# Spreading 1/sum of the softmax with a float32r one-hot product in two parts instead of a float32 one

## The chip, the cores and the metric

The kernel runs on one core of one Trainium2 chip, as one program launch. The metric is the device time of that launch in microseconds (us), and a profile is one further execution of the same program.

## The reference, cut to what matters

A hybrid encoder of two layers over 512 tokens of width 1024, then a final RMSNorm. In each layer one input projection feeds a bidirectional SSD (Mamba-2) group and a grouped-query attention group (8 query heads, 2 key/value heads, 64 wide); their outputs are concatenated, go through one output projection and are added to the residual, and a SwiGLU feed-forward follows. What the change touches is the division in the softmax:

```
s = jnp.einsum("bqgrd,bkgd->bgrqk", qi, k)
p = jax.nn.softmax(s, axis=-1)
out = jnp.einsum("bgrqk,bkgd->bqgrd", p, v)
```

The kernel keeps exp(s - max) without the division, multiplies it by v, and divides the 512 x 512 attention output by the row sums at the end.

## The kernel before, in words

Weights and activations are split in a high and a low float32r tile (`whi`, `wlo`, `xh`, `xl`), and a product is three float32r matmuls: high by high (L410), high by low (L411), low by high (L412), 512 columns each. `Stream.split` makes the two weight tiles from each fetched chunk: a cast on ScalarE (L191) and a subtraction on VectorE (L192).

In `mixer` three generators are interleaved: `att` (attention), `fill` (the projections, and `out_half(1)`, the half of the output projection that uses the SSD group's rows) and `ssd`. Attention leaves unnormalized outputs in `qr` and the row sums in `sums` (128 tokens x 4 chunks x 8 heads). When the projections are done, `att` calls `normalize` at high priority:

- `sel`, 8 x 512, has a 1 where column / 64 equals the row, made by GpSimd with a memset (L676) and a select (L678) in a slot of the ring `p_ring`.
- `rec` = 1/sums on VectorE (L681), four transposes on TensorE into a bank `ps_t` (L684), a ScalarE copy to `rows`, 8 x 512 (L686), another slot of `p_ring`.
- For each j of 4, a float32 matmul of a 128-column piece of `sel` by `rows` (L689) spreads 1/sum over 128 partitions into one of two banks `ps_s`. VectorE multiplies `qr` by it (L691), ScalarE casts the product to `xh` (L693), and VectorE subtracts for `xl` (L694, a call of the helper `tt`, so that its records stand under L94).

Then `out_half(0)` multiplies these four row blocks: each output block m takes three matmuls for each of k = 0 to 3, and block k needs the `xh` and `xl` that pass j = k made. Sums leave the two banks `ps_a` by a VectorE addition (L820). The last matmuls of `out_half(1)` and the first of `out_half(0)` stand beside the four passes of `normalize`.

The order in which each engine gets its instructions isn't written by hand: the program is traced with a planner (`schedule_with_timeline_sim=True` at the end of the file) that simulates each engine with its own costs and picks the next instruction by priority and readiness. Each engine then runs its list in order.

Of the kernel before, what the change touches and what calls it, by code (L numbers as in the profile page):

```python
# [15 lines left out]
F32 = mybir.dt.float32  # L16
F32R = mybir.dt.float32r
I32 = mybir.dt.int32
AF = mybir.ActivationFunctionType
ALU = mybir.AluOpType  # L20
# [3 lines left out]
P = 128  # L24
# [3 lines left out]
S = 512  # L28
NC = S // P
# [17 lines left out]
B1, B2, B3, BR = 2, 2, 3, 2  # L47
# [22 lines left out]
def merge(a, b, c):  # L70
    return a.rearrange("p (b c) -> p b c", b=b, c=c)


def bc(ap, shape, axis):
    return ap.unsqueeze(axis).broadcast_to(shape)
# [3 lines left out]
def tile_hybrid_encoder(ctx, tc, xt_d, par_d, rope_d, snw_d, w_kvdt, w_xbc, w_q, w_z, w_out, w_gate, w_up, w_down, out_d):  # L79
    nc = tc.nc  # L80
    V, A, G, T = nc.vector, nc.scalar, nc.gpsimd, nc.tensor
# [11 lines left out]
    def tt(e, *args):  # L93
        (G if e == "G" else V).tensor_tensor(*args)  # L94

    def bank(tag):


        return psum.tile([P, S], F32, name=f"ps_{tag}", tag=tag)
# [151 lines left out]
    ident = const.tile([P, P], F32, name="ident")  # L251
# [184 lines left out]
    def mixer(l, norm, mx):  # L436
# [26 lines left out]
        for c in range(NC):  # L463
            out = A.activation(kvd[:, c], pk[c][:, :KVDT], AF.Copy, scale=rt[:, c:c + 1])  # L464
# [6 lines left out]
        base = mx.tile([P, 2, NC, 64], F32, name="base", tag="t2", bufs=B2)  # L471
# [29 lines left out]
        if l == 0:  # L501
            for t, rows, v in ((segr, (0, 32), 1.0), (segl, (64, 72), -1.0)):
                hot = mx.tile([P, 8], F32, name="hot", tag="qm", bufs=2)
                G.memset(hot, 0.0)
                for r in rows:
                    G.affine_select(out=hot, in_=hot, pattern=[[-1, 8]], compare_op=ALU.not_equal, fill=v,
                                    base=-r, channel_multiplier=1)
# [144 lines left out]
        def ring(which):  # L652
            turn[which] += 1
            return rings[which][:, turn[which] % 4]
# [15 lines left out]
        sums = mx.tile([P, NC, 8], F32, name="sums")  # L670

        def normalize():


            sel = ring("p")[:8]
            G.memset(sel, 0.0)  # L676
            pick = merge(sel, 8, 64)
            G.affine_select(out=pick, in_=pick, pattern=[[-1, 8], [0, 64]], compare_op=ALU.not_equal, fill=1.0,  # L678
                            base=0, channel_multiplier=1)
            rec = mx.tile([P, NC, 8], F32, name="rec")  # L680
            V.reciprocal(rec, sums)  # L681
            tp = bank("t")
            for c in range(NC):
                T.transpose(tp[:8, c * P:(c + 1) * P], rec[:, c], ident)  # L684
            rows = ring("p")[:8]
            A.copy(rows, tp[:8])  # L686
            for j in range(4):
                b = bank("s")
                T.matmul(b, lhsT=sel[:, j * P:(j + 1) * P], rhs=rows, start=True, stop=True)  # L689
                o = qr.rearrange("p c (j a) d -> p j c (a d)", a=2)[:, j]  # L690
                V.tensor_tensor(o, o, merge(b, NC, P), ALU.mult)  # L691
                h = merge(mixed.h[j], NC, P)
                A.copy(h, o)  # L693
                tt(MLE, merge(mixed.l[j], NC, P), o, h.bitcast(F32), ALU.subtract)  # L694
# [191 lines left out]
        def att():  # L886
            todo = [(c, g) for g in range(2) for c in range(NC)]
            ready = None
            for i, (c, g) in enumerate(todo):
                while g not in qri:  # L890
                    yield
                now = ready or queries(c, g)
                ready = None
                if i + 1 < len(todo) and todo[i + 1][1] in qri:
                    ready = queries(*todo[i + 1])
                yield from attention(c, g, *now)
            while "z" not in done:
                yield
            with tc.high_priority():
                normalize()  # L900
            done.append("att")
# [290 lines left out]
```

## Time and profile before

| | us |
|---|---|
| median of 3 runs shown | 1235.92 |
| the three runs | 1235.92, 1230.69, 2627.81 |
| the profiled execution's own time | 1231.69 |
| its span, first to last instruction | 1230.0 |
| TensorE busy | 1198.6 (97%) |
| VectorE busy | 902.4 (73%) |
| ScalarE busy | 630.5 (51%) |
| GpSimd busy | 157.8 (13%) |
| mean granted TensorE clock | 0.990 of full speed |

PE is TensorE's matmuls, PEld its weight loads, DVE VectorE, ACT ScalarE, POOL GpSimd. Matmuls are pipelined, so the duration of one record is longer than the distance from its start to that of the next; the chain of waits counts the distance. A float32 matmul leaves two records, a float32r one a single record. Times in the traces count from the span's start. `normalize` runs once in each layer, near 209 to 244 us and 808 to 843 us.

### The profile page before, as it was taken

How to read it: one execution, taken by the hardware profiler on the slowest of the kernel's cores; microseconds unless marked ns; L12 is line 12 of the kernel's file. 1: busy time of each engine (PE TensorE's matmuls, PEld its weight loads, DVE VectorE, ACT ScalarE, POOL GpSimd, SP SyncE). 2: the span in 40 equal slices, each digit the busy share in tenths (PEclk: the TensorE clock that was granted, in tenths of full speed). 3: DMA queues.
4: the chain of work that ended last, by engine and by line, in shares of the span. 5: the costliest groups of instructions: out<-in, count | busy, mean ns of one | idle time of the engine just before them, and what ended most of it. 6: DMA issues, size and time to landing. Idle time of an engine off the chain costs nothing.

```text
span 1230.0 us, 19740 instructions
## 1 busy us (share of the span) xinstructions
PE 1198.6 (97%) x7718; PEld 1059.6 (86%) x7718; DVE 902.4 (73%) x1475; ACT 630.5 (51%) x1203; POOL 157.8 (13%) x144
## 2 busy tenths in 40 slices
PE   6999999999999999999999999999999999999996
PEld 6788886687899899899898898777879989989985
DVE  6898976457887677677679977856698847847843
ACT  5678675244354254254465776744444623623544
POOL 0203433011100000000202144401020000000002
PEclk9999999999999999999999999999999999999998
DMA  6221212224243234231442111212243333333121
GB/s 224 73 73 48 66 37 68 69 69 142 89 126 120 65 120 126 64 104 39 126 147 91 69 35 61 87 35 69 77 146 112 105 110 95 102 114 95 35 72 75
DMA packets 47534, 110.04 MB, mean 89 GB/s; under 512 B 5425, under 2 KB 5937, under 8 KB 47441
## 3 DMA queue, kind: packets, MB, share of 16 engines
q1 hardware_dynamic: 46720, 107.68, 27.7%
q8 instruction: 60, 0.98, 0.3%
q10 hardware_dynamic: 720, 1.11, 0.3%
q14 instruction: 34, 0.27, 0.1%
HBM read 104.44 MB, written 4.33 MB: 88 GB/s over the span
## 4 chain that ended last, share of the span: by engine, by line
PE 86%; DVE 9%; ACT 2%; issue 1%; DMA 1%; POOL 0%; ACTq 0%; DVEq 0%; POOLq 0%
PE ps_a L1054 6%; PE ps_a L1053 6%; PE ps_a L1052 6%; PE ps_a L410 5%; PE ps_a L411 5%; PE ps_a L412 5%; PE ps_a L1099 3%; PE ps_a L1098 3%; PE ps_a L1100 3%; PE ps_s L1098 3%; PE ps_s L1099 3%; PE ps_s L1100 3%; PE ps_s L1054 3%; PE ps_s L1053 3%; PE ps_s L1052 3%; PE ps_t L717 3%
## 5 line engine op out<-in xcount | busy, mean ns | idle before, releaser
L191 ACT CAST whi<-wraw 128x512 fp32r<-128x512 f32 (+4 forms) x183 | 125.5, 714 | 217.7 <-PE ps_a L411 57.6
L191 ACT CAST whi<-sraw 128x1024 fp32r<-128x1024 f32 x126 | 131.6, 1050 | 141.2 <-DVE sraw L166 40.7
L192 DVE TENSOR_TENSOR wlo<-wraw,whi 128x512 fp32r<-128x512 f32 (+4 forms) x183 | 152.5, 845 | 59.5 <-ACT whi L191 58.4
L192 DVE TENSOR_TENSOR wlo<-sraw,whi 128x1024 fp32r<-128x1024 f32 x126 | 153.5, 1223 | 46.5 <-ACT whi L191 46.3
L410 PE MATMUL ps_a<-xh,whi 128*128 128x512 f32 x320 | 128.3, 405 | 5.5 <-ACT kvd L464 1.7
L411 PE MATMUL ps_a<-xl,whi 128*128 128x512 f32 x320 | 128.2, 402 | 0.0
L412 PE MATMUL ps_a<-xh,wlo 128*128 128x512 f32 x320 | 127.8, 399 | 0.0
L322 POOL TENSOR_TENSOR ssq<-ssq,sqt 128x512 f32<-128x512 f32 x17 | 25.2, 1481 | 671.1 <-ACT sqt L319 670.8
L166 DVE TENSOR_TENSOR sraw<-sraw 128x1024 f32<-128x1024 f32 x72 | 88.0, 1222 | 1.0
L418 PE MATMUL ps_a<-whi,xh 128*128 128x256 f32 (+1 forms) x256 | 74.6, 292 | 9.4 <-ACT xh L306 9.4
L1054 PE MATMUL ps_a<-ss,wlo 128*128 128x256 f32 x288 | 81.7, 284 | 0.0
L1052 PE MATMUL ps_a<-ss,whi 128*128 128x256 f32 x288 | 81.5, 283 | 0.0
L1053 PE MATMUL ps_a<-ss,whi 128*128 128x256 f32 x288 | 81.5, 283 | 0.0
L1054 PE MATMUL ps_a<-s,wlo 128*128 128x256 f32 x288 | 81.1, 283 | 0.0
L1053 PE MATMUL ps_a<-s,whi 128*128 128x256 f32 x288 | 81.1, 283 | 0.0
L410 PEld LDWEIGHTS ps_a<-xh,whi 128*128 128x128 f32 x320 | 61.6, 193 | 22.1 <-ACT s L1013 4.0
L1052 PE MATMUL ps_a<-s,whi 128*128 128x256 f32 x288 | 79.8, 283 | 0.0
L411 PEld LDWEIGHTS ps_a<-xl,whi 128*128 128x128 f32 x320 | 61.4, 192 | 15.5 <-DVE xl L94 1.5
L419 PE MATMUL ps_a<-wlo,xh 128*128 128x256 f32 (+1 forms) x256 | 74.2, 291 | 0.0
L412 PEld LDWEIGHTS ps_a<-xh,wlo 128*128 128x128 f32 x320 | 61.4, 192 | 14.7 <-issue 2.0
L420 PE MATMUL ps_a<-whi,xl 128*128 128x256 f32 (+1 forms) x256 | 72.5, 287 | 0.0
L1098 PE MATMUL ps_s<-hid,whi 128*128 128x512 f32 (+1 forms) x182 | 69.9, 384 | 0.0
(399 smaller groups left out, 3420.4 us busy)
## 6 DMA issues: line engine op xcount, KB each, us to landing
sraw<-in_w_gate SPq DMA_DIRECT2D x72, 256.0 KB, 5.6
sraw<-in_w_up SPq DMA_DIRECT2D x72, 256.0 KB, 4.2
wraw<-in_w_down SPq DMA_DIRECT2D x48, 384.0 KB, 3.5
wraw<-in_w_xbc SPq DMA_DIRECT2D x16, 512.0 KB, 3.3
wraw<-in_w_out SPq DMA_DIRECT2D x16, 512.0 KB, 4.2
wraw<-in_w_q SPq DMA_DIRECT2D x8, 512.0 KB, 3.3
wraw<-in_w_z SPq DMA_DIRECT2D x8, 512.0 KB, 3.4
wraw<-in_w_gate SPq DMA_DIRECT2D x8, 512.0 KB
```

Of the source, the lines that this page charges most:

```text
L166: V.tensor_tensor(q[to], q[to], q[by], ALU.add)
L191: A.copy(hi[:, u], raw[:, u])
L192: (G if lo_pool else V).tensor_tensor(lo[:, u], raw[:, u], hi[:, u].bitcast(F32), ALU.subtract)
L410: T.matmul(ps, lhsT=wh, rhs=op.h[k], start=first, stop=False)
L411: T.matmul(ps, lhsT=wh, rhs=op.l[k], start=False, stop=False)
L412: T.matmul(ps, lhsT=wl, rhs=op.h[k], start=False, stop=last)
L418: T.matmul(ps, lhsT=xh, rhs=wh, start=first, stop=False)
L419: T.matmul(ps, lhsT=xh, rhs=wl, start=False, stop=False)
L1052: T.matmul(out, lhsT=wh[:, o:o + P], rhs=x_[:, 0, i], start=first and i + j == 0, stop=False, skip_group_check=True)
L1053: T.matmul(out, lhsT=wh[:, o:o + P], rhs=x_[:, 1, i], start=False, stop=False, skip_group_check=True)
L1054: T.matmul(out, lhsT=wl[:, o:o + P], rhs=x_[:, 0, i], start=False, stop=i == 3, skip_group_check=True)
L1098: T.matmul(ps[:, cols], lhsT=w1[:, o:o + P], rhs=h, start=f == a, stop=False)
```

## The change

`sel` is built on VectorE as a sum of two broadcast pieces of the identity: rows 0 to 7 and rows 8 to 15 each hold the one-hot pattern, 16 x 512, in float32r, in a buffer of the tag `raw`, which the convolution and the query projection use earlier. 1/sum is split in a float32r part and the rest (`rec` is 128 x 4 x 16): the reciprocal is taken in place, a VectorE copy rounds it, a VectorE subtraction gives the rest. The four transposes give 16 rows instead of 8, the ScalarE copy writes 16 x 512 in float32r into the other `raw` buffer, and the four matmuls at L689 contract 16 rows in float32r. The two GpSimd instructions are gone. Nothing else is edited.

```diff
         def normalize():
-            sel = ring("p")[:8]
-            G.memset(sel, 0.0)
-            pick = merge(sel, 8, 64)
-            G.affine_select(out=pick, in_=pick, pattern=[[-1, 8], [0, 64]], compare_op=ALU.not_equal, fill=1.0,
-                            base=0, channel_multiplier=1)
-            rec = mx.tile([P, NC, 8], F32, name="rec")
-            V.reciprocal(rec, sums)
+            sel = mx.tile([P, S + 4], F32R, name="one", tag="raw", bufs=BR)[:16, :S]
+            V.tensor_tensor(merge(sel, 8, 64), bc(ident[:16, :8], [16, 8, 64], 2), bc(ident[:16, 8:16], [16, 8, 64], 2), ALU.add)
+            rec = mx.tile([P, NC, 16], F32R, name="rec")
+            V.reciprocal(sums, sums)
+            V.tensor_copy(rec[:, :, :8], sums)
+            V.tensor_tensor(rec[:, :, 8:], sums, rec[:, :, :8].bitcast(F32), ALU.subtract)
             tp = bank("t")
             for c in range(NC):
-                T.transpose(tp[:8, c * P:(c + 1) * P], rec[:, c], ident)
-            rows = ring("p")[:8]
-            A.copy(rows, tp[:8])
+                T.transpose(tp[:16, c * P:(c + 1) * P], rec[:, c].bitcast(F32), ident)
+            rows = mx.tile([P, S + 4], F32R, name="rows", tag="raw", bufs=BR)[:16, :S]
+            A.copy(rows, tp[:16])
             for j in range(4):
                 b = bank("s")
                 T.matmul(b, lhsT=sel[:, j * P:(j + 1) * P], rhs=rows, start=True, stop=True)
```

## Rows read from the trace of the kernel before

**Rows 1.** The page, part 1: busy time, share of the span, instructions.
```profile
PE 1198.6 (97%) x7718; PEld 1059.6 (86%) x7718; DVE 902.4 (73%) x1475; ACT 630.5 (51%) x1203; POOL 157.8 (13%) x144
```

**Rows 2.** Windows of both layers: us, busy (count) PE PEld DVE ACT POOL, PEclk, DMA, GB/s.
```profile
235.30:250.30 15.00, 14.67 (x39) 8.22 (x37) 7.79 (x13) 4.11 (x7) 0.00 (x0) 0.77 0.11 36
834.50:847.90 13.40, 13.07 (x39) 7.60 (x37) 7.72 (x13) 4.14 (x7) 0.00 (x0) 0.87 0.12 39
```

**Rows 3.** The chain of waits: start us, us on the chain, what.
```profile
235.67 1.91 PE ps_s L689 x4
...
238.01 0.23 PE ps_a L410
...
238.71 1.05 PE ps_s L689 x2
...
240.19 1.81 PE ps_s L689 x2
...
243.16 0.43 PE ps_a L410
...
834.86 1.91 PE ps_s L689 x4
...
839.38 1.05 PE ps_s L689 x2
```

**Rows 4.** Timeline, TensorE: start us, us, engine, line, operation, out<-in, shapes, count.
```profile
235.60 1.98 PE L689 MATMUL ps_s<-p_ring 8*128 8x512 f32 x4
...
238.31 0.40 PE L412 MATMUL ps_a<-xh,wlo 128*128 128x512 f32 x1
...
243.38 0.63 PE L411 MATMUL ps_a<-xl,whi 128*128 128x512 f32 x1
...
249.50 0.39 PE L412 MATMUL ps_a<-xh,wlo 128*128 128x512 f32 x1
...
834.79 1.98 PE L689 MATMUL ps_s<-p_ring 8*128 8x512 f32 x4
...
841.22 0.63 PE L411 MATMUL ps_a<-xl,whi 128*128 128x512 f32 x1
...
847.08 0.39 PE L412 MATMUL ps_a<-xh,wlo 128*128 128x512 f32 x1
```

**Rows 5.** Timeline, VectorE, same columns; [idle before <-what ended it].
```profile
236.76 0.69 DVE L691 TENSOR_TENSOR qr<-qr,ps_s 128x512 f32<-128x512 f32 x1 [2.17 <-PE ps_s L689]
...
238.83 0.68 DVE L820 TENSOR_TENSOR part<-part,ps_a 128x512 f32<-128x512 f32 x1
...
241.23 0.68 DVE L94 TENSOR_TENSOR xl<-qr,xh 128x512 fp32r<-128x512 f32 x1
...
242.65 1.51 DVE L94 TENSOR_TENSOR xl<-qr,xh 128x512 fp32r<-128x512 f32 x2
...
835.95 0.69 DVE L691 TENSOR_TENSOR qr<-qr,ps_s 128x512 f32<-128x512 f32 x1 [2.18 <-PE ps_s L689]
...
840.42 0.69 DVE L94 TENSOR_TENSOR xl<-qr,xh 128x512 fp32r<-128x512 f32 x1
```

**Rows 6.** Windows in which TensorE's clock was low; columns as in rows 2.
```profile
242.00:246.80 4.80, 4.80 (x13) 3.75 (x12) 1.98 (x3) 0.62 (x1) 0.00 (x0) 0.50 0.33 109
841.20:844.20 3.00, 3.00 (x8) 2.32 (x7) 1.80 (x3) 0.62 (x1) 0.00 (x0) 0.50 0.53 175
```

**Rows 7.** Timeline, TensorE, early in layer 0: the first matmul after a stall.
```profile
32.59 0.80 PE L410 MATMUL ps_a<-xh,whi 128*128 128x512 f32 x1 [1.66 <-ACT kvd L464]
```

**Rows 8.** VectorE, by line and tile (ns min/median/max, first and last start), then one timeline row.
```profile
L681 DVE RECIPROCAL rec<-sums x2: 353/353/353, 210.9 to 808.7; 128x32 f32<-128x32 f32 x2
...
L94 DVE TENSOR_TENSOR H<-H,EX x8: 681/1054/1342, 134.4 to 746.4; 128x512 f32<-128x512 f32 x8
L740 DVE TENSOR_TENSOR H<-H,ps_m x8: 674/680/687, 135.5 to 748.3; 128x512 f32<-128x512 f32 x8
...
212.33 0.69 DVE L820 TENSOR_TENSOR part<-part,ps_a 128x512 f32<-128x512 f32 x1 [1.08 <-PE ps_a L412]
```

## The prediction, as put on record before the result

> **What bounds the kernel now.** The page's busy times come first: TensorE has work in 97% of the span, VectorE in 73% [rows 1]. An edit that takes nothing from TensorE's list, or from a wait on it, can't show. The windows around `normalize` come next, one in each layer: 15.0 and 13.4 us, in which TensorE still looks busy throughout, but at a granted clock of 0.77 and 0.87 [rows 2]. So these two windows, 28.4 us together, are where the change can act, and busy time alone doesn't tell what they hold.
>
> The chain of waits does. In it the eight records of L689 take 1.91, 1.05 and 1.81 us in layer 0 and 1.91, 1.05 and again 1.05 us in layer 1 [rows 3]: 4.77 + 4.01 = 8.78 us for eight products. Beside them one float32r matmul of 512 columns takes 0.23 us on the chain at the full clock and 0.43 us at the low one [rows 3]. A float32 product here is about four times as dear as a float32r one (1.91 us for two).
>
> The third view is VectorE's timeline in the same window. From the first L691 at 236.76 us to the end of the pair of L94 at 244.16 us it works nearly back to back, 7.40 us for eleven instructions [rows 5]. In layer 1 the piece from the first L691 to the end of the second L94 is 5.16 us, in layer 0 5.15 [rows 5]. So under TensorE's float32 passes lies a VectorE chain almost as long, and it is what will be late next.
>
> **The change part by part.** I make the sum against the profiled execution's own 1231.69 us (span 1230.0). The median of the three runs shown is 1235.92, the lowest 1230.69; the profile is near the low one, and 5.2 us lie between these two, so a gain of a few us is close to what two runs differ by.
>
> The products. Eight float32r products cost 8 x 0.23 = 1.84 us against 8.78: 6.9 us less on TensorE. Sixteen contracted rows instead of eight I cost at nothing: the duration goes with the 512 columns, since L410 with 128 rows has the 0.23 us.
>
> What of it reaches the end. I place three points in each layer, counted from the start of the first product (235.60 and 834.79 [rows 4]). First L691 starts 1.16 us after it, since it waits for two float32 records [rows 4, 5]. After a single float32r matmul VectorE starts 0.52 us later (L412 at 238.31, L820 at 238.83 [rows 4, 5]). That brings VectorE's chain 0.64 us forward. Second, the fifth matmul of `out_half(0)`, an L411, needs the second L94. Now it starts at +7.78 us in layer 0 and +6.43 in layer 1 [rows 4]; the second L94 could be over at 0.52 + 5.15 = +5.67. TensorE's own work ahead of that point (four products and eight float32r matmuls, 12 x 0.23 = 2.8 us) is shorter, so VectorE sets it. Gains: 2.11 and 0.76 us, 2.87 together. Third, from there to the start of the 24th matmul there are 19 steps, now 6.12 and 5.86 us [rows 4], since part of them run at half clock: 4.8 and 3.0 us are seen at 0.50 [rows 6]. At the full clock they would take 19 x 0.23 = 4.37, 3.24 us less over both layers. VectorE's last L94, at +7.92, wouldn't stop that: the six matmuls that need block 3 would start near +8.9.
>
> Does the clock come back? Before it fell, TensorE had float32 passes with gaps of up to 0.8 us between groups; early in layer 0 it is also low right after a stall of 1.66 us [rows 7]. After the change TensorE has 2.8 us of work in the first 5.67, against 6.43 to 7.78 well-filled ones, so it idles more, not less. I take the low clock to stay as long as now, and the third gain as zero. The two ends are 0 and 3.24.
>
> The new VectorE work. `sel` adds two SBUF operands over 512 columns. Its nearest rows are the products of H: 0.68 to 1.34 us, median 1.05, where the form with a PSUM operand never passes 0.69 [rows 8]. That first form is slow when GpSimd works beside it, I take it. The Trainium skill says the same as a rule, in SBUF — State Buffer, section Who interferes with whom: a VectorE instruction with two SBUF inputs and a GpSimd instruction that reads SBUF share a port as an exclusive lock, so one waits for the whole of the other. By that rule the shift from GpSimd to VectorE could cost up to 1.34 us a layer and hold GpSimd too; by the fastest row it costs 0.68. The copy and the subtraction over 128 x 32 are bounded by the reciprocal of that shape, 0.353 us each [rows 8]. Together 0.68 + 0.2 to 1.34 + 0.71 = 2.05 us a layer. I cost them at nothing: `sel` depends on no result of the layer but a free buffer, and behind the reciprocal VectorE sits idle 1.08 us waiting for the projection's sums [rows 8], while TensorE runs `out_half(1)`. If that cover is gone (the planner puts `sel` in front of a wait of TensorE's), the price is up to 2 x 2.05 = 4.1 us.
>
> The rest has one answer: GpSimd's two instructions go and nobody waited for them, four transposes load 16 columns instead of 8, the ScalarE copy has the same 512 columns, no DMA is added or moved. The `raw` buffers were last read by the query projection, long before. Sum: 1231.69 - 2.87 = 1228.8 us, say 1229.
>
> **The rivals.**
>
> *The clock stays up.* If TensorE's shorter list lets it run the 19 steps at 0.23 us, both gains count: 2.87 + 3.24 = 6.1, 1225.6 us. For it: the low stretch in layer 1 is shorter (3.0 against 4.8 us) where the window was denser. Against: the idle time grows. Its lowest value: if the planner also moves VectorE's L820 and L192 behind `normalize`, all 6.9 us of products and the 3.24 are gained, 1221.5.
>
> *Slower: TensorE starves and the low clock covers everything.* With quick products TensorE waits for VectorE in several short pieces before the second L94. If the clock falls there and the 19 steps all run at 0.43 us, they end at 5.67 + 8.17 = +13.84, against +13.90 now in layer 0 and +12.29 in layer 1: 1.5 us slower, and up to 4.1 more where the new VectorE work is on the path, 1233.2 to 1237.3. It decides in layer 1, where more than eleven of the 19 steps at 0.43 us (4.37 + 11 x 0.2 = 6.6 us) use up the 0.76 us won; now it is about seven (5.86 us). The skill has a rule for this, in TensorE: Matmul & The Clock Gate, section A second HAM failure mode: psum-queue depth-cycling: frequent short idles between groups of matmuls that cycle through PSUM banks make the clock swing and cost throughput. The low clock in both layers agrees with it; no row shows it for float32r products.
>
> *No change.* The planner picks an order with its own costs, and may put other work ahead of the products, or another wait of `out_half(0)` (its weights' cast and subtraction) may stand where the products stood: 1231.7. That the product isn't faster at all would give the same; against it stands every float32r record with 0.23.
>
> **How the numbers follow.** Forecast 0.45, clock stays up 0.2, slower 0.2, no change 0.15. The likeliest gives 1229. The range takes in the lowest value of the clock rival, 1221, and the top of the slower one, 1237.3, hence 1221 to 1238; a different order elsewhere in the layers, which the planner may give, is what I leave out. A measurement of this kernel can tell about 2%, 24.7 us, from no change. No case comes near; only a rearranged layer could, equally to both sides: faster 0.02, within 0.96, slower 0.02.
>
> **What would show it.** Each product one record of some 0.4 us, 0.23 on the chain; the first L691 about 0.5 us after the first product; TensorE waiting for VectorE at the fifth matmul of `out_half(0)`; the two windows 12.9 and 12.6 us long, with a clock still under 1 in both. A clock of 1.00 there speaks for the first rival; longer low stretches than 4.8 and 3.0 us for the second. I'm wrong if the windows don't shrink, if `sel` or the split stands in front of a TensorE wait, or if the time moves in stretches where nothing was edited.

## The result and the profile after

The changed kernel takes 1219.45 us (median of 6 runs), the kernel before 1235.1 in the runs beside it: ratio 0.9883, 95% interval 0.9853 to 0.9913, so 1.2% faster. Some executions took far longer (one of 2627.81 us of the kernel before, the profiled one of e9 with 3018.6 us), and the ratios leave them out. The forecast was 1229, the range 1221 to 1238. The direction was right, the time under the range, and the gain four to five times the 2.87 us of the forecast: 12.0 us between the two profiled executions (spans of 1218.0 and 1230.0 us), 14.4 us by the ratio.

The page after, part 1 (columns as in [rows 1]):

```profile
PE 1186.2 (97%) x7710; PEld 1055.1 (87%) x7710; DVE 904.1 (74%) x1481; ACT 629.1 (52%) x1203; POOL 157.1 (13%) x140
```

TensorE has eight records less, one for each product. To see where the 12 us are, I cut both traces at events that no edit touches: in layer 0 from the first product of the SSD states (L731 of the kernel before) to the first matmul of `product` in the feed-forward (L1052), and in layer 1 from the first write of the convolution's input (L592) to that same matmul. The text calls these events the SSD states, the convolution and the feed-forward. The windows of the kernel before (us, busy and count of PE, PEld, DVE, ACT, POOL, then granted clock, DMA share, GB/s):

```profile
132.70:335.70 203.00, 197.93 (x1103) 158.65 (x1102) 143.84 (x250) 102.58 (x211) 44.98 (x37) 0.98 0.25 78
640.60:933.30 292.70, 288.69 (x1705) 238.35 (x1704) 230.40 (x443) 167.72 (x387) 69.68 (x57) 0.99 0.24 77
```

and of the changed one:

```profile
131.70:324.10 192.40, 188.85 (x1096) 155.56 (x1095) 143.34 (x251) 101.82 (x211) 44.78 (x35) 1.00 0.26 83
629.00:921.70 292.70, 286.23 (x1700) 238.06 (x1699) 231.74 (x446) 167.90 (x387) 68.41 (x55) 0.99 0.24 77
```

Layer 0 is 10.6 us shorter, layer 1 not at all. The other 1.4 us lie outside these windows: the convolution of layer 0 starts at 40.1 instead of 41.6 us, and over all kernels of this study whose traces are cut so it lies between 38.9 and 41.6, with no edit before it.

In layer 1 the seam looks as a rival had it. TensorE and VectorE in the changed kernel's timeline there (start us, us, then as in [rows 4, 5]):

```profile
825.77 0.72 PE L688 MATMUL ps_s<-rows,one 16*128 16x512 f32 x2
826.31 1.28 DVE L690 TENSOR_TENSOR qr<-qr,ps_s 128x512 f32<-128x512 f32 x2 [1.55 <-PE ps_s L688]
829.60 0.50 PE L411 MATMUL ps_a<-xl,whi 128*128 128x512 f32 x1 [0.67 <-DVE xl L94]
832.00 0.50 PE L411 MATMUL ps_a<-xl,whi 128*128 128x512 f32 x1 [0.73 <-DVE xl L94]
835.54 0.39 PE L412 MATMUL ps_a<-xh,wlo 128*128 128x512 f32 x1
```

L690 starts 0.54 us after the first product (1.16 before), TensorE waits for VectorE's `xl` until +3.8 and +6.2 us (at the third and ninth matmul of `out_half(0)`, not at the fifth), and the 24th matmul starts at +9.77 us, 2.5 us earlier than at +12.29 [rows 4]. The window of this seam, against 13.40 us at a clock of 0.87 [rows 2]:

```profile
825.70:836.30 10.60, 8.87 (x34) 5.65 (x33) 7.57 (x13) 3.88 (x7) 0.00 (x0) 1.00 0.13 49
```

The clock stays at its upper level, 2.4 GHz, though TensorE idles more than before. But layer 1 as a whole has gained nothing: about 2.6 us were lost ahead of the seam, where the clock dips in a stretch that kept it before.

In layer 0 the picture is another one. VectorE after, the new instruction, and the additions of `out_half(1)` (eight) with the first of `out_half(0)`:

```profile
120.40 1.26 DVE L676 TENSOR_TENSOR one<-ident 16x512 fp32r<-16x512 f32 x1
...
219.30 0.68 DVE L819 TENSOR_TENSOR part<-part,ps_a 128x512 f32<-128x512 f32 x1
...
233.47 0.69 DVE L819 TENSOR_TENSOR part<-part,ps_a 128x512 f32<-128x512 f32 x1 [2.03 <-PE ps_a L412]
236.19 0.69 DVE L819 TENSOR_TENSOR x<-part,ps_a 128x512 f32<-128x512 f32 x1 [0.82 <-PE ps_a L412]
```

TensorE in the same kernel has the products at 214.19 and 218.90 us:

```profile
214.19 0.73 PE L688 MATMUL ps_s<-rows,one 16*128 16x512 f32 x2
...
218.90 0.73 PE L688 MATMUL ps_s<-rows,one 16*128 16x512 f32 x2
```

Behind the last product, TensorE's list still has five of the eight blocks of `out_half(1)`; before, not one sum was left behind the last product (the last one, L820 at 238.83, stands ahead of it [rows 5]). The instruction order of layer 0 is different: attention is over earlier (the reciprocal starts at 202.1 us, against 210.9 [rows 8]), so some 14 us of dense matmuls of `out_half(1)`, from 219.6 to 233.3 us, are left to lie beside what `normalize` still has to do. The transposes of 1/sum ran at 229.26 us before, 18 us after the reciprocal, with TensorE busy on other work in between; now they run at 208.57 us, 6 us after it. From 209 to 236 us nothing is idle on TensorE:

```profile
209.00:236.00 27.00, 27.00 (x127) 21.29 (x126) 15.22 (x24) 7.77 (x14) 0.00 (x0) 1.00 0.18 59
```

### The profile page after: what moved, and what is told of

Read it like the earlier page. It is cut to its first block, busy times and chain, and to the rows that moved or that the text cites. A ratio compares the mean times of both kernels' runs of the same rounds, so it can differ in the third digit from the quotient of the medians.

```text
span 1218.0 us, 19728 instructions
## 1 busy us (share of the span) xinstructions
PE 1186.2 (97%) x7710; PEld 1055.1 (87%) x7710; DVE 904.1 (74%) x1481; ACT 629.1 (52%) x1203; POOL 157.1 (13%) x140
## 4 chain that ended last, share of the span: by engine, by line
PE 86%; DVE 9%; ACT 2%; issue 1%; DMA 0%; POOL 0%; ACTq 0%; DVEq 0%; POOLq 0%
PE ps_a L1053 6%; PE ps_a L1052 6%; PE ps_a L1051 6%; PE ps_a L410 5%; PE ps_a L411 5%; PE ps_a L412 4%; PE ps_a L1097 3%; PE ps_a L1098 3%; PE ps_a L1099 3%; PE ps_s L1097 3%; PE ps_s L1098 3%; PE ps_s L1099 3%; PE ps_s L1053 3%; PE ps_s L1052 3%; PE ps_s L1051 3%; PE ps_t L716 3%
## 5 line engine op out<-in xcount | busy, mean ns | idle before, releaser
L1052 PE MATMUL ps_a<-ss,whi 128*128 128x256 f32 x288 | 81.5, 283 | 0.0
L1052 PE MATMUL ps_a<-s,whi 128*128 128x256 f32 x288 | 81.1, 283 | 0.0
```

Of the source, the lines that this page charges most:

```text
L1052: T.matmul(out, lhsT=wh[:, o:o + P], rhs=x_[:, 1, i], start=False, stop=False, skip_group_check=True)
```

## The experiments

Theory A: quick products at the seam make the whole gain. Theory B: most of it is the planner's other order in layer 0, set off by the new VectorE instruction near 120 us, and what the order gives is cover for `normalize`, that is, matmuls of other work that run while its steps on VectorE and ScalarE are under way. The letters C, D and E in the expectations are narrower rivals. All results stand together here: median and ratio from timed runs, the two stretches (from the SSD states to the feed-forward in layer 0, from the convolution to the feed-forward in layer 1) from each profiled execution.

| | us, median | ratio to before (95%) | layer 0 | layer 1 |
|---|---|---|---|---|
| before | 1231 to 1235 | | 203.0 | 292.7 |
| changed | 1219.45 | 0.9883 (0.9853 to 0.9913) | 192.4 | 292.7 |
| e1 product alone | 1224.0 | 0.9927 (0.9905 to 0.9949) | 198.9 | 290.1 |
| e2 one-hot rows alone | 1222.86 | 0.9922 (0.9898 to 0.9946) | 194.9 | 292.6 |
| e3 idle VectorE instruction | 1225.01 | 0.9942 (0.9920 to 0.9965) | 194.9 | 298.4 |
| e4 changed, late attention first | 1216.05 | 0.9863 (0.9839 to 0.9887) | 192.5 | 288.3 |
| e5 order alone | 1223.47 | 0.9929 (0.9908 to 0.9951) | 198.6 | 290.3 |
| e6 order and product | 1219.35 | 0.9893 (0.9874 to 0.9913) | 196.0 | 287.8 |
| e7 changed, four blocks first | 1215.88 | 0.9864 (0.9842 to 0.9886) | 192.4 | 288.3 |
| e8 float32 in the new order | 1224.11 | 0.9948 (0.9923 to 0.9972) | 194.9 | 293.6 |
| e9 one-hot rows late | 1230.44 | 0.9985 (0.9976 to 0.9995) | | |
| e10 one-hot rows by layer | 1217.65 | 0.9879 (0.9863 to 0.9896) | 192.4 | 290.0 |
| e11 e10, late first in layer 1 | 1214.25 | 0.9859 (0.9839 to 0.9878) | 192.3 | 287.0 |

**e1, the product without VectorE's one-hot rows.** Against the changed kernel:

```diff
-            V.tensor_tensor(merge(sel, 8, 64), bc(ident[:16, :8], [16, 8, 64], 2), bc(ident[:16, 8:16], [16, 8, 64], 2), ALU.add)
+            raw01 = ring("p")[:16]
+            G.memset(raw01, 0.0)
+            pick = merge(raw01, 8, 64)
+            G.affine_select(out=pick, in_=pick, ..., base=0, channel_multiplier=1)
+            G.affine_select(out=merge(sel, 8, 64), in_=pick, ..., base=-8, channel_multiplier=1)
```

> The float32r product in two parts alone: as in the changed kernel, but GpSimd builds the one-hot rows (a memset and two selects in a slot of p_ring, the last one writing float32r), so VectorE gets no early instruction. Theory A (the gain comes from the quick products at the seam between the two halves of the output projection): all of the gain is kept, about 1219 us. Theory B (most of the gain comes from the planner's other order in layer 0, which the new VectorE instruction near 120 us sets off): layer 0 keeps the order of before, with the products behind nearly all of out_half(1); only the two seams get shorter, by about 2.5 us each, so about 1226 us, 5 us below before.

1224.0 us. The windows of the two layers, and of the two seams:

```profile
131.90:330.80 198.90, 192.42 (x1099) 156.16 (x1098) 144.03 (x252) 102.39 (x211) 45.61 (x38) 1.00 0.25 80
635.70:925.80 290.10, 284.69 (x1701) 236.58 (x1700) 231.04 (x445) 167.43 (x387) 69.96 (x58) 1.00 0.24 77
...
829.80:840.30 10.50, 8.78 (x34) 5.63 (x33) 7.54 (x13) 3.85 (x7) 0.00 (x0) 1.00 0.15 50
234.80:245.40 10.60, 8.87 (x34) 5.68 (x33) 7.60 (x13) 3.92 (x7) 0.00 (x0) 1.00 0.15 52
```

Both seams have the same length and a clock of 1.00, and the stretches win 4.1 and 2.6 us. This is the change as the prediction thought of it, and the 6.7 us that it wins in these stretches are near the 6.1 of the rival in which the clock stays up (by the medians of the timed runs it wins 8.2 us, and 1224.0 lies 2 us under theory B's figure). In both layers no sum of `out_half(1)` comes after the last product. e1 also puts its one-hot rows in a `raw` buffer, so taking that buffer isn't what gives layer 0 its other order.

**e2, the one-hot rows alone.** Against the kernel before:

```diff
-            sel = ring("p")[:8]
-            G.memset(sel, 0.0)
+            sel = mx.tile([P, S + 4], F32, name="one", tag="raw", bufs=BR)[:8, :S]
...
-            G.affine_select(out=pick, ...)
+            V.tensor_copy(merge(sel, 8, 64), bc(ident[:8, :8], [8, 8, 64], 2))
```

> The other part alone: VectorE copies the one-hot rows from the identity (8 rows, float32) into a raw buffer, 1/sum and the four products stay float32 as before. Theory A: no gain, 1231 to 1235 us as before, at most 1.5 us slower for the VectorE copy. Theory B: the order of layer 0 is that of the changed kernel (products with half of out_half(1) still to come), so about 7 to 8 us faster than before, 1223 to 1225 us; layer 1 keeps its slow seam, with a low clock.

1222.86 us with every product still in float32. Its windows:

```profile
131.30:326.20 194.90, 191.43 (x1100) 156.16 (x1100) 144.00 (x249) 102.04 (x211) 44.37 (x35) 1.00 0.26 82
631.10:923.70 292.60, 288.58 (x1704) 238.43 (x1703) 232.02 (x443) 167.55 (x387) 69.14 (x55) 0.99 0.24 77
...
825.20:838.90 13.70, 13.37 (x40) 8.10 (x40) 8.26 (x14) 4.71 (x8) 0.00 (x0) 0.88 0.12 38
```

Layer 0 wins 8.1 us, layer 1 nothing, and its seam keeps its low clock (0.88). The chain of waits still has the float32 passes at full price, in layer 0 too:

```profile
213.86 1.91 PE ps_s L686 x4
...
219.85 1.91 PE ps_s L686 x4
```

So theory A falls: the products are as dear as before, and layer 0 has three quarters of its gain.

**e3, an instruction that nobody reads.** Against the kernel before, at the head of `normalize`:

```diff
+            dm = mx.tile([P, S + 4], F32, name="one", tag="raw", bufs=BR)[:16, :S]
+            V.tensor_tensor(merge(dm, 8, 64), bc(ident[:16, :8], [16, 8, 64], 2), bc(ident[:16, 8:16], [16, 8, 64], 2), ALU.add)
```

> The kernel before with one VectorE instruction added that nobody reads: the sum of two identity pieces, 16 x 512, into a raw buffer, at the place where normalize begins. GpSimd's one-hot rows and the float32 products stay. Theory A: no gain, 1231 to 1237 us, since work was only added. Theory B: the same order of layer 0 as in the changed kernel and 7 to 8 us faster than before, 1223 to 1225 us, though not one edit of the change that matters is in it.

1225.01 us: work was added and the kernel became faster. Windows, the two layers and 5 us of layer 1:

```profile
132.00:326.90 194.90, 191.36 (x1100) 156.32 (x1099) 144.05 (x250) 101.93 (x211) 46.10 (x37) 1.00 0.26 82
631.90:930.30 298.40, 293.33 (x1703) 241.94 (x1703) 231.59 (x443) 168.09 (x387) 69.95 (x57) 0.98 0.24 75
...
780.00:785.00 5.00, 5.00 (x25) 4.76 (x24) 1.50 (x4) 1.09 (x3) 3.95 (x4) 0.55 0.59 162
```

Layer 0 is 194.9 us as in e2. Layer 1 of this execution lost 5.7 us, with the clock at 0.55 near 780 us, which nobody expected.

**e9, the same rows, but late.** As e2, with `sel = ring("p")[:8]` kept, whose slot comes free only when attention nears its end.

> The one-hot rows alone by VectorE (8 rows, float32, float32 products), but in a slot of p_ring instead of a raw buffer. The slot comes free only near the end of attention, so the instruction can't run early. Theory B as sharpened (it is an instruction early in VectorE's list, near 120 us, that makes the planner finish attention sooner in layer 0): layer 0 keeps its slow order, the stretch from the state products to the feed-forward stays at 203 us; 1228 to 1233 us in all. Theory D (building the rows on VectorE instead of GpSimd helps by itself): about 8 us faster, 1223.

1230.44 us, 0.15% below before. VectorE builds the rows and next to nothing is gained. No stretch is given for e9, but its trace has the order of before: in layer 0 the last product stands behind all eight sums of `out_half(1)`, and VectorE's copy starts just ahead of the reciprocal. With e2 and e3, where the instruction starts at 120.1 and 120.7 us, this says that it isn't what the instruction does but that it can run early that gives layer 0 its order.

**e4 and e7, more of attention ahead.** In `att`, the changed kernel with the last three (e7: four) attention blocks of a layer at high priority (e4 spells the same loop in other words):

```diff
-                yield from attention(c, g, *now)
+                if i + 3 < len(todo):
+                    yield from attention(c, g, *now)
+                    continue
+                gen, end = attention(c, g, *now), False
+                while not end:
+                    with tc.high_priority():
+                        end = next(gen, "end") == "end"
+                    if not end:
+                        yield
```

> The changed kernel, with the last three of the eight attention blocks of each layer traced at high priority, so that attention ends sooner and normalize comes with more of out_half(1) still to run, in both layers. Theory A: as the changed kernel, 1219 us. Theory B: layer 1 gains what layer 0 gained by its order, some 3 to 8 us: 1211 to 1216 us.

> The changed kernel with the last four, not three, attention blocks at high priority. Theory B: as with three, 1215 to 1217 us; a difference beyond 2 us would mean that the exact order counts, not only the cover. Theory A: 1219 us as the changed kernel.

1216.05 and 1215.88 us; the windows of e4:

```profile
132.20:324.70 192.50, 190.04 (x1096) 156.09 (x1095) 143.45 (x251) 101.96 (x211) 44.06 (x35) 1.00 0.26 83
629.60:917.90 288.30, 284.55 (x1700) 237.27 (x1699) 231.45 (x445) 168.56 (x387) 68.82 (x55) 1.00 0.25 78
```

Layer 1 now has two sums of `out_half(1)` behind its products and wins 4.4 us; three or four blocks make no difference. For e4 the window given was 1211 to 1216, so it came at its edge.

**e5 and e6, order without and with the product.** The same edit on the kernel before (e5), and on e1 (e6).

> The kernel before, whole (GpSimd's one-hot rows, float32 products), with only the last three attention blocks of each layer traced at high priority, so that the products come with about half of out_half(1) still to run in both layers. Theory B (what counts is the work of out_half(1) left on TensorE as cover for normalize): both layers gain, 6 to 12 us below before, 1220 to 1226 us, and no low clock at the seams. Theory C (the VectorE instruction moved something else in layer 0 that made it shorter, and cover is not the cause): no gain, 1230 to 1233 us.

> The float32r products in two parts with GpSimd's one-hot rows (the first experiment) and the last three attention blocks at high priority: order and product together, without any added VectorE instruction of 512 columns. Theory B: about 1 to 2.5 us a layer below the order alone, 1214 to 1219 us, near the changed kernel with late attention first (1216). Theory C: as the product alone, 1224 us.

1223.47 and 1219.35 us. The windows of e5:

```profile
130.60:329.20 198.60, 194.85 (x1103) 157.53 (x1102) 143.69 (x249) 103.10 (x211) 44.94 (x37) 1.00 0.25 80
634.10:924.40 290.30, 286.75 (x1705) 238.16 (x1704) 230.24 (x442) 168.56 (x387) 69.28 (x57) 1.00 0.24 77
```

and of e6:

```profile
132.40:328.40 196.00, 192.25 (x1099) 156.80 (x1098) 144.38 (x251) 102.90 (x211) 45.55 (x38) 1.00 0.25 81
633.30:921.10 287.80, 284.25 (x1701) 237.46 (x1700) 231.26 (x446) 168.33 (x387) 69.66 (x58) 1.00 0.25 78
```

e5 contains neither part of the change and wins 4.4 and 2.4 us, so cover is worth something by itself; e6 came 0.35 us above its window. In both, two sums of each layer come after the products, and the clock is 1.00. With float32 products, layer 0 takes 203.0, 198.6 and 194.9 us as 0, 2 and 5 sums follow the last product (before, e5, e2); with float32r ones 198.9, 196.0 and 192.4 as 0, 2 and 5 follow (e1, e6, changed).

The last step of these rows, from 2 to 5, isn't shown to be cover, and theory C falls only in part. The stretch from the SSD states to the first matmul of `out_half(1)`, before, in e2 and in e5:

```profile
132.70:209.10 76.40, 73.25 (x557) 61.10 (x556) 60.35 (x129) 53.48 (x140) 30.25 (x29) 1.00 0.20 60
131.30:207.50 76.20, 74.42 (x584) 62.51 (x583) 60.48 (x129) 55.44 (x146) 30.21 (x28) 1.00 0.20 60
130.60:209.40 78.80, 76.64 (x581) 63.29 (x579) 61.10 (x131) 56.06 (x144) 30.79 (x30) 1.00 0.19 58
```

In the same time as before, TensorE gets 27 records more done in e2 (the end of attention, which before stands between the matmuls of `out_half(1)`); e5 gets nearly as many done as e2, but needs 2.6 us more for them (against before, 2.4 us more for 24 more records, so what e5 wins lies behind this stretch). So e2's 8.1 us are the 4.4 that e5 wins as well and 3.7 more, most of which come from this stretch, ahead of `out_half(1)`, into which more of attention fits.

**e8, float32 in the new order.** The changed kernel with `F32` for `one`, `rec` and `rows`.

> The changed kernel with float32 tiles for the 16 one-hot rows, for 1/sum and for the products, so that each product leaves two records again, while the instruction order of layer 0 stays that of the changed kernel. Theory A: the gain is lost, about 1231 us. Theory B: only the products' own passes come back, 2.5 us in layer 0 (where they lie among dense matmuls) and 0 to 3 us at the seam of layer 1: 1222 to 1225 us.

1224.11 us, 194.9 us in layer 0: the product's own worth in that order is 2.5 us. In layer 1 the seam has its low clock back, with sixteen contracted rows:

```profile
827.60:842.00 14.40, 14.07 (x43) 8.58 (x43) 8.90 (x14) 5.34 (x9) 0.00 (x0) 0.88 0.11 36
```

**e10 and e11, the best of each layer.** e10 takes VectorE's one-hot rows `if l == 0` and GpSimd's (as in e1) in layer 1; e11 has the edit of e7 in layer 1 alone as well.

> The changed kernel with the one-hot rows by VectorE in layer 0 and by GpSimd in layer 1. Theory B: layer 0 as in the changed kernel (192.4 us from the state products to the feed-forward), layer 1 as with the product alone (290.0 us from the convolution to the feed-forward, instead of 292.7), so some 2 to 3 us below the changed kernel: 1216 to 1218 us. Theory E (the 2.7 us that layer 1 of the changed kernel lost ahead of its seam was a matter of one execution and not of its order): as the changed kernel, 1219 to 1220.

> As the tenth, and in layer 1 the last four attention blocks at high priority: the best order seen for each layer. Theory B: layer 0 at 192.4 us and layer 1 near 287.5 us, 1213 to 1215 us, 1 to 3 us below the fastest so far (1216).

1217.65 and 1214.25 us. The windows of e11:

```profile
131.20:323.50 192.30, 188.76 (x1096) 155.60 (x1095) 143.34 (x252) 101.93 (x211) 44.83 (x35) 1.00 0.26 83
628.50:915.50 287.00, 283.87 (x1699) 237.26 (x1699) 230.54 (x444) 167.93 (x387) 69.60 (x58) 1.00 0.25 78
```

In the profile of e10 the stretch of layer 1 is 290.0 us, as in e1, so the 2.7 us lost in the changed kernel are not lost without the VectorE instruction there. But the instruction doesn't bring the loss by itself: from the convolution to the first product, layer 1 takes 196.7 us in the changed kernel and 194.0 in e10, but also 194.1 in e2 and 195.0 in e8, which have a VectorE instruction at that place too. The timed runs don't settle it: the ratio 0.9879 lies inside the interval of the changed kernel. e11 has the lowest median of all, 5.2 us under the changed kernel's, in other runs; its interval (0.9839 to 0.9878) overlaps the lower part of that of the changed kernel.

## Why the prediction was wrong

**Which engine sets the seam: right.** TensorE's float32 passes hid a VectorE chain nearly as long. After the change TensorE waits for `xl` twice, and the first L690 starts 0.54 us after the first product, where 0.52 was forecast. The products' price was near: two take 0.66 us on the chain, 0.33 each where 0.23 was forecast, and 1.91 before.

**The clock: wrong.** I took the low clock to stay because TensorE would idle more. It idles more and stays at 1.00 in both seams of e1 and in that of layer 1 after the change. With the float32 passes the clock fell again at layer 1's seam, in e2 with eight contracted rows (0.88) and in e8 with sixteen (0.88). So at these seams float32 passes, not idle time and not the number of rows, went with the fall. The gaps of up to 0.8 us that the prediction gave as a sign stand in no record of TensorE's matmuls there: in the kernel before it is busy from 235.60 to 242.00 us:

```profile
235.60:242.00 6.40, 6.40 (x15) 2.19 (x14) 4.98 (x8) 2.90 (x5) 0.00 (x0) 0.87 0.01 3
```

Nor do the short idles of the slower rival show before the fall; where they do show, behind float32r products, the clock stayed up. Taking the third gain of 3.24 us as zero was the mis-set term; with it the sum was 6.1 us, and e1 won 6.7 in its two stretches.

**"A different order elsewhere in the layers ... is what I leave out": this step failed most.** I costed `sel` at nothing since "it depends on no result of the layer but a free buffer". For the same reason it could run at 120 us, 94 us ahead of the products that read it, and the planner, which simulates each engine, gave the end of attention, `normalize` and `out_half(1)` of layer 0 another order. That is 8.1 of layer 0's 10.6 us (e2, e3); the products give the other 2.5 (192.4 against 194.9 in e8). The prediction's own sign of being wrong, time that moves where nothing was edited, came up. And its first rule, that an edit must take something from TensorE's list or from a wait on it, doesn't guard against this: e3 only adds work to VectorE, and TensorE's list changes all the same.

**What the order gives: seen too narrowly.** The prediction took the place of `normalize`, behind nearly all of `out_half(1)`, as given, and priced only the chain there. A large part of the cost of `normalize` was that nothing was left on TensorE to hide it. e5 shows it with neither part of the change: 4.4 and 2.4 us. Most of that may be the clock: 15.00 us at 0.77 and 13.40 us at 0.87 [rows 2] lose an estimated 3.5 and 1.7 us against the full clock, which e5 keeps. Most of the other 3.7 us of layer 0's 8.1 come from the attention work that fits in ahead of `out_half(1)`, and why it fits is not shown.

**New VectorE work: too low.** The sum for `sel` takes 1.26 and 1.52 us in the two layers, the second over the bound of 1.34; 0.18 and 0.19 us for the copy and the subtraction lie inside theirs, and both hide as thought. In layer 1, `sel` runs early too (at 706.5 us) and bought no better order. The changed kernel lost 2.6 us there ahead of the seam, but e2 and e8 lost 0 and 0.8 us with an instruction at the same place, so the price of `sel` itself is not shown.

**Rivals and chances.** "The clock stays up" happened at the seam, "No change" in layer 1 as a whole, and the largest part came from a case that I named and left without a price.

**Open.** Why an early VectorE instruction lets the planner finish attention sooner in layer 0 and not in layer 1 is not shown; that it does is (e2, e3, and not e1, e9). Nor is it shown what lets the clock dip near 775 us of layer 1 in the changed kernel and near 780 in e3, but not in e1, e2 or before at the corresponding place:

```profile
775.00:780.00 5.00, 3.60 (x16) 2.98 (x15) 3.52 (x7) 1.73 (x5) 2.17 (x2) 0.73 0.66 220
```

is the changed kernel, and the kernel before has, about 10 us later in its own time, a similar dip in TensorE's work without one in the clock:

```profile
785.00:790.00 5.00, 3.68 (x26) 2.90 (x24) 4.74 (x7) 2.24 (x7) 2.33 (x3) 1.00 0.75 234
```

## What to carry to other kernels

Where a planner sets the order, an instruction that depends on nothing isn't free: price a reordering of everything behind it in both directions, and to tell it from the edit's own worth, add the instruction alone, unread. Before a serial step at a seam is made faster, ask whether it can run while the work ahead of it still fills the engine: here moving it there (e5) won as much as the faster product alone (e1) in layer 0, 4.4 and 4.1 us. And a step's time on an engine that is 97% busy is only worth what the next wait leaves of it; count that wait first.

## What was not expected of the hardware

A stretch with float32 matmuls and few others was followed by the lower clock, though TensorE's records show hardly any idle time in it (0.77 and 0.87 over the seams with eight contracted rows [rows 2], 0.88 in e2, and 0.88 in e8 with sixteen), while the same seam with float32r matmuls of sixteen rows and 1.73 us of TensorE idle in 10.60 kept 1.00. In e5, float32 products between dense matmuls kept 1.00 as well.
